# An HGRN2 layer on one core: block sums, a gate projection and residual steps in another place

## The chip, the core and the metric

The kernel runs on one core of one Trainium2 chip. A core has a matrix engine (TensorE, PE in the profile; its weight loads are listed apart as PEld), and VectorE (DVE), ScalarE (ACT), GpSimd (POOL) and SyncE (SP), which here issues all the transfers. Each engine takes its instructions in order from a queue of its own and waits on semaphores for the others. The metric is the device time of one execution in microseconds; lower is better.

## What is computed

A backbone of two layers over 512 latent tokens and 256 context tokens of width 1024. Layer 0 is a half-step SwiGLU, a bidirectional HGRN2 mixer and another half-step SwiGLU; layer 1 has a chunked MLP in the mixer's place. The change lies in the mixer of layer 0 and in the residual ahead of it:

```python
def post_norm_update(x, y, m, k, g, b):
    return layer_norm(DN_ALPHA * x + m[..., 3 * k + 2, :] * y, g, b)

def hgrn2_project(h, w_in, lb):
    p = (h @ w_in).astype(jnp.float32)
    p = p.reshape(bsz, length, 5, HG_HEADS, HG_DK).transpose(2, 0, 3, 1, 4)
    q = jax.nn.silu(p[0])
    i = p[1]
    lbb = lb[:, None]
    f = lbb + (1 - lbb) * jax.nn.sigmoid(p[2:4])
    return q, i, 1 - f, jnp.log(f), p[4]
...
    # gla_chunkwise, forward and reversed, over context and then latent tokens
    b = jnp.cumsum(logf, axis=-2)
    q_in = q * jnp.exp(b)
    k_in = k * jnp.exp(-b)
    scores = jnp.where(lower, jnp.einsum('nbhtd,nbhsd->nbhts', q_in, k_in), 0.0)
    o_intra = jnp.einsum('nbhts,nbhse->nbhte', scores, v)
...
    o = o * lax.rsqrt(jnp.mean(o * o, axis=-1, keepdims=True) + RMS_EPS) * norm_w
    o = o * jax.nn.silu(g)
```

`q` are the queries, `p[2:4]` the two forget gates (one for each direction), `i` the values and `g` the output gate, for each of 8 heads of width 128.

## The kernel before

**Precision and operands.** Every large product is made of three matmuls (`mm3`, L152 to L154): each operand is held as a high half, rounded by ScalarE (`split`, L139), and a low half, the difference, made by VectorE (L140). So a weight block costs one ACT and one DVE step beside its load. `unit` (L145) loads a block of 512 KB into one of three buffers `raw` and splits it into one of six buffers `w`. The features lie on the partitions: `xa` holds the 768 tokens for the mixer, the latent ones first.

**Values.** All values of the mixer (`i` above) are made ahead of the heads, by `HgrnValues`: a product of 2 x 2 blocks by seven block products in place of eight. The input is cut into four blocks, (feature half, token half), each 512 features by 384 tokens. Four of the products take sums of them, f5, f6, f7 and f4, in this order, and weights that are sums as well (`e`, `u`). `rest` (L984 on) makes these four products; each `next(steps)` in it emits the next of the sums, which `sum_steps` (L854 on, of a class shared with another phase) adds in place in `held`: one block addition is two DVE adds (L863), one sum's operand is two splits. L990 and L996 add products into values, L998 makes the last weight sums. Ahead of them stand the projections of head 0 to its queries and its gate (`proj_silu`, L1495 to L1505: 24 matmuls into `psq`, three ACT steps and a DVE product).

**Heads.** The loop over heads (from h = 0) works on two heads at once: it projects for head h and runs the scores and states of head h - 1. `proj_forget` (L1560 on) makes one direction's gates: `psfl` for the latent and `psfc` for the context tokens, clipped into `X` (L1568, L1569), then a chain to and fro between ScalarE and VectorE: L1575 (ACT), two logarithms, the differences L1576 and L1577 (DVE), the running sum by a scan (L1581), small steps, six L1594 (DVE) and L1595 (ACT) that finish `X`, the scaled keys, and L1597 (DVE), L1598 (ACT), L1605 (DVE, `queries`) that finish the scaled queries in `B`. TensorE then transposes the keys (`ptk`, L1611), makes the near scores (`pssn`, L1623, eight instances of 128 by 128, which read the queries and `kkn`), the far scores (`pssc`, L1634), the context states (`pkc`, L1643, read by DVE at L1650), the latent ones and the outputs (`po`, L1696 on). The transposes ahead of head 0's scores take the context keys of both directions first.

**Residual.** The input of post_norm_update for the mixer is x1 = ALPHA * (z1 * g + b), the output of the first half-step's layer norm, and is needed again only behind the mixer. `settle` (L1714 on) makes it at h = 0 right behind the first forget projection: for each half of the 1024 features a row load of g and of b (L1719, L1720), then for each of four token tiles a load of z (L1723), two DVE steps (L1724, L1725) and a store (L1726). The rows lie in the two buffers `kT` of the heads, z in their three `tmp`.

**Order.** The order of each engine's queue is decided when the kernel is built: a scheduler orders the instructions by their dependencies, buffers and the order in which the code emits them. A load into a buffer waits for the last reader of what lay there, and as SyncE's queue is in order, all transfers behind it wait too.

Of the kernel before, what the change touches and what calls it, by code (L numbers as in the profile page):

```python
# [19 lines left out]
P = 128  # L20
D = 1024
KD = D // P
T = 512
# [51 lines left out]
def backbone_kernel(  # L75
# [804 lines left out]
            put(self.f4, (0, 0))  # L880
            yield

    class HgrnValues(BothSums, Phase):


        hold = False
# [75 lines left out]
        def fifth(self):  # L962

            for c in range(2):
                nc.vector.tensor_tensor(self.e[c], self.g0[c], self.u[0][c], ALU.subtract)
            self.we = [self.weights(e) for e in self.e]

        def rest(self, steps):

# [526 lines left out]
    def proj_silu(h, idx, tag):  # L1496

        w = unit(hg_wf[idx, h])
        ps = bank("psq")
        last = feat_mm(ps, w, xm, 0, T)  # L1500
        o = qg.tile([P, T], F32, tag=tag, name=tag, bufs=1)
        nc.scalar.activation(o, ps, AF.Exp, scale=-1.0)
        nc.scalar.activation(o, o, AF.Ln, bias=one)
        nc.scalar.activation(o, o, AF.Exp, scale=-1.0)
        nc.vector.tensor_tensor(o, ps, o, ALU.mult)  # L1505
        return o, last

    with sbuf(name="vs", bufs=1) as vs:
        hv.f7, hv.f4, hv.f6, hv.f5 = (vs.tile([P, 2, KD // 2, TS], F32R, name=f"f{i}") for i in (7, 4, 6, 5))
        q0, g0 = proj_silu(0, 0, "q"), proj_silu(0, 3, "g")  # L1510
        hv.rest(hv.sum_steps())
    vw.close()

    with sbuf(name="hgo", bufs=1) as hgo, ExitStack() as late:
        hts = [hgo.tile([P, 2, T], F32R, name=f"ht{h}") for h in range(NH - NLATE)]
        hgo2 = late.enter_context(swap("hgo2"))
        hts.extend(hgo2.tile([P, 2, T], F32R, name=f"ht{h}") for h in range(NH - NLATE, NH))

        with sbuf(name="hg", bufs=1) as hg:
            mask = []  # L1520
            for d in range(2):
# [189 lines left out]
                lambda t: x1[t], True, (0, 2), None, lambda t: x2[t], f2, tail=4,  # L1711
            )

            def settle():  # L1714

                for hf in range(2):
                    c = slice(hf * HC, (hf + 1) * HC)
                    g, b = (hg.tile([P, NT, P], F32, tag="kT", name="kT", bufs=2).rearrange("p s t -> p (s t)") for _ in range(2))
                    nc.sync.dma_start(g, ln_g[0, 0][c].partition_broadcast(P))  # L1719
                    nc.sync.dma_start(b, ln_b[0, 0][c].partition_broadcast(P))  # L1720
                    for t in range(NT):
                        z = hg.tile([P, NT, P], F32, tag="tmp", name="z", bufs=3).rearrange("p s t -> p (s t)")
                        nc.sync.dma_start(z, z1[t][:, c])  # L1723
                        nc.vector.scalar_tensor_tensor(z, z, ALPHA, g, ALU.mult, ALU.mult)  # L1724
                        nc.vector.scalar_tensor_tensor(z, b, ALPHA, z, ALU.mult, ALU.add)  # L1725
                        nc.sync.dma_start(x1[t][:, c], z)  # L1726

            prev, made_of, g, last = None, None, None, None
            for h in range(NH + 1):
                if h < NH:  # L1730
                    n0, last, _ = proj_forget(h, 0)
                    if h == 0:
                        settle()
                else:
                    op.lead(0, 1)
                done = None
                if made_of:
                    with tc.issue_after(last.ins):
                        done = (made_of[0], outputs(*made_of), g)
                if prev:  # L1740
                    r0, r1 = prev
                    kTc = transposed([r.kk[:, NT + s, :] for r in prev for s in range(NTC)])
                    kT0 = transposed([r0.kk[:, s, :] for s in lat_order(0)[:-1]])
                    near_scores(r0)
                    far_scores(0, r0)
                if h < NH:
                    n1, _, last = proj_forget(h, 1)
                if done and h < NH:
                    with tc.issue_after(last.ins):
                        gated(*done)  # L1750
                if prev:
                    context_states(h - 1, prev, kTc)
                    kT1 = transposed([r1.kk[:, s, :] for s in lat_order(1)[:-1]])
                    latent_states(h - 1, 0, r0, kT0)
                    far_scores(1, r1)
                if h < NH:
                    q, last = proj_silu(h, 0, "q") if h else q0
                    if prev:

                        with tc.issue_after(last.ins):  # L1760
                            latent_states(h - 1, 1, r1, kT1)
                    for r in (n0, n1):
                        queries(r, q)
                else:
                    latent_states(h - 1, 1, r1, kT1)
                    op.lead(0, 2)
                    gated(*done)
                if prev:
                    made_of = (h - 1, prev)
                    if h == NH:  # L1770
                        on = outputs(*made_of)
                    g, last = proj_silu(h - 1, 3, "g") if h > 1 else g0
                if h < NH:
                    prev = (n0, n1)
# [271 lines left out]
```

## Time and profile before

| | us |
|---|---|
| three runs | 2413.31, 2415.90, 2416.14 (median 2415.9) |
| the profiled execution | 2413.81 |
| its span, first to last instruction | 2412.1 |
| mean granted TensorE clock | 0.998 |

The same, by stretches around the place of the change: length, busy time of TensorE, VectorE, ScalarE, granted clock, share of the transfer engines.

| stretch | us | PE | DVE | ACT | clock | DMA |
|---|---|---|---|---|---|---|
| plain value products, 500 to 560 | 60 | 59.17 | 47.11 | 23.09 | 1.00 | 0.32 |
| q and g of head 0, start of f5's and f6's, 560 to 587 | 27 | 27.00 | 26.60 | 22.09 | 1.00 | 0.13 |
| the other value products, forget gates of head 0, 587 to 637 | 50 | 50.00 | 35.75 | 20.93 | 1.00 | 0.59 |
| transposes and near scores of head 0, 637 to 651 | 14 | 6.10 | 11.64 | 7.01 | 0.76 | 0.37 |
| heads 0 and 1, 651 to 700 | 49 | 48.78 | 43.53 | 22.77 | 1.00 | 0.15 |

A row of the profile reads: start and duration in us of one instruction or of a run of the same ones, engine, line, operation, output and inputs by their names in the program, shape, count. What stands in brackets behind it is how long the engine idled just before and what released it: the engine, the tile and its line. A row without a start is a group: busy time, mean in ns, then idle before it. DMA issues are listed with their count, KB of each, and the median us from issue to landing.

### The profile page before, as it was taken

The numbers are of one execution on the slowest core, as the hardware profiler recorded it, in microseconds if no ns is written. First come the engines' busy times: TensorE is split into PE (matmuls) and PEld (weight loads), VectorE is DVE, ScalarE is ACT, GpSimd is POOL, SyncE is SP. The second block draws the span as 40 slices with busy tenths as digits, with TensorE's granted clock in tenths as the row PEclk, the third lists the DMA queues.
The fourth block names the chain that finished last, engine by engine and source line by source line (L and its number), as shares of the span: only waits on it lengthen the run. The fifth ranks groups of instructions, "written<-read, shape, count | busy, mean of one in ns | idle before, by whom it ended". The sixth has DMA issues, their size and how long they took to land.

```text
span 2412.1 us, 37626 instructions
## 1 busy us (share of the span) xinstructions
PE 2378.3 (99%) x14791; PEld 2183.0 (91%) x14791; DVE 2011.2 (83%) x3203; ACT 1197.3 (50%) x1861; POOL 35.6 (1%) x58
## 2 busy tenths in 40 slices
PE   7999999999899999999999999999999999999998
PEld 5899998888788988999988999889999988999987
DVE  7997797868788887988897988898888787988785
ACT  4544433336445443555534655544666543555641
POOL 0000000000000000000000000000000000000000
PEclk9999999999999999999999999999999999999999
DMA  7443489842411224433584333673332374333451
GB/s 302 169 162 125 137 293 379 289 159 82 151 57 52 63 62 147 138 106 106 176 263 155 106 106 115 202 227 135 99 103 88 123 251 151 132 109 105 146 164 73
DMA packets 110196, 362.05 MB, mean 150 GB/s; under 512 B 12681, under 2 KB 14913, under 8 KB 110018
## 3 DMA queue, kind: packets, MB, share of 16 engines
q1 hardware_dynamic: 110018, 359.65, 44.3%
q8 instruction: 115, 1.88, 0.3%
q14 instruction: 63, 0.52, 0.1%
HBM read 336.25 MB, written 23.36 MB: 149 GB/s over the span
## 4 chain that ended last, share of the span: by engine, by line
PE 87%; DVE 7%; DMA 2%; ACT 1%; issue 1%; POOL 0%; SPq 0%; DVEq 0%; POOLq 0%; ACTq 0%
PE y L152 9%; PE y L153 9%; PE y L154 9%; PE psc L152 7%; PE psc L154 7%; PE psc L153 7%; PE pse L154 3%; PE pse L152 3%; PE pse L153 3%; PE psa L152 2%; PE psa L154 2%; PE psa L153 2%; PE psf L152 2%; PE psf L154 2%; PE psf L153 2%; DVE w L140 1%
## 5 line engine op out<-in xcount | busy, mean ns | idle before, releaser
L139 ACT ACTIVATE w<-raw 128x1024 fp32r<-128x1024 f32 (+3 forms) x391 | 369.9, 949 | 377.8 <-DMA raw<-in_ffn_w_out 142.1
L140 DVE TENSOR_TENSOR w<-raw,w 128x1024 fp32r<-128x1024 f32 (+3 forms) x391 | 424.4, 1089 | 101.0 <-ACT w L139 100.4
L152 PE MATMUL y<-w,hs 128*128 128x512 f32 x976 | 380.7, 390 | 0.0
L154 PE MATMUL y<-w,hs 128*128 128x512 f32 x976 | 379.8, 389 | 0.0
L153 PE MATMUL y<-w,hs 128*128 128x512 f32 x976 | 379.8, 389 | 0.0
L152 PEld LDWEIGHTS y<-w,hs 128*128 128x128 f32 x976 | 183.2, 188 | 38.3
L154 PEld LDWEIGHTS y<-w,hs 128*128 128x128 f32 x976 | 183.2, 188 | 38.3
L153 PEld LDWEIGHTS y<-w,hs 128*128 128x128 f32 x976 | 183.2, 188 | 37.4
L152 PE MATMUL psc<-f,w 128*128 128x256 f32 (+1 forms) x680 | 199.1, 293 | 0.0
L154 PE MATMUL pse<-f,w 128*128 128x256 f32 (+1 forms) x680 | 198.9, 292 | 0.1
L152 PE MATMUL pse<-f,w 128*128 128x256 f32 (+1 forms) x680 | 198.7, 292 | 0.2 <-ACT sc L770 0.2
L153 PE MATMUL pse<-f,w 128*128 128x256 f32 (+1 forms) x680 | 198.6, 292 | 0.0
L154 PE MATMUL psc<-f,w 128*128 128x256 f32 (+1 forms) x680 | 198.5, 292 | 0.0
L153 PE MATMUL psc<-f,w 128*128 128x256 f32 (+1 forms) x680 | 198.5, 292 | 0.0
L770 ACT ACTIVATE sc<-psc 128x256 f32<-128x256 f32 (+1 forms) x235 | 94.6, 402 | 148.3 <-PE psc L154 136.7
L152 PE MATMUL psc<-xm,w 128*128 128x256 f32 x548 | 156.3, 285 | 1.6 <-ACT sc L770 1.6
L154 PE MATMUL psc<-xm,w 128*128 128x256 f32 x548 | 155.1, 283 | 0.0
L153 PE MATMUL psc<-xm,w 128*128 128x256 f32 x548 | 155.0, 283 | 0.0
L140 DVE TENSOR_TENSOR w<-rawu,w 128x1024 fp32r<-128x1024 f32 x85 | 103.9, 1223 | 46.8 <-ACT w L139 46.8
L152 PEld LDWEIGHTS psc<-f,w 128*128 128x128 f32 x680 | 130.0, 191 | 0.8 <-ACT sc L770 0.6
L154 PEld LDWEIGHTS pse<-f,w 128*128 128x128 f32 x680 | 130.0, 191 | 0.7 <-DVE w L140 0.7
L152 PEld LDWEIGHTS pse<-f,w 128*128 128x128 f32 x680 | 130.0, 191 | 0.4 <-ACT sc L770 0.4
(441 smaller groups left out, 6152.1 us busy)
## 6 DMA issues: line engine op xcount, KB each, us to landing
raw<-in_ffn_w_in SPq DMA_DIRECT2D x114, 512.0 KB, 4.6
raw<-in_ffn_w_out SPq DMA_DIRECT2D x88, 512.0 KB, 4.4
rawu<-in_ffn_w_in SPq DMA_DIRECT2D x75, 512.0 KB, 3.5
rawu<-in_mod_w SPq DMA_DIRECT2D x72, 512.0 KB, 4.2
mraw<-in_mod_w SPq DMA_DIRECT2D x56, 512.0 KB, 4.8
hl<-hd SPq DMA_DIRECT2D x44, 384.0 KB, 5.5
raw<-in_hg_wf SPq DMA_DIRECT2D x32, 512.0 KB, 3.9
x<-x SPq DMA_DIRECT2D x28, 512.0 KB, 4.1
```

Of the source, the lines that this page charges most:

```text
L139: latest_hi[0] = nc.scalar.activation(dst_hi, src, AF.Copy)
L140: latest[0] = nc.vector.tensor_tensor(dst_lo, src, dst_hi.bitcast(F32), ALU.subtract)
L152: nc.tensor.matmul(ps, ah, bh, start=start, stop=False, **kw)
L153: nc.tensor.matmul(ps, ah, bl, start=False, stop=False, **kw)
L154: return nc.tensor.matmul(ps, al, bh, start=False, stop=stop, **kw)
L770: self.copies.append(nc.scalar.activation(sc[i], ps[:, :N2], AF.Copy, scale=scale))
```

## The change

Three parts, all around the values and head 0. The line numbers of the changed kernel are higher by 24 to 29 behind the first part: L863 is L977 in the new function, L1568 is L1594, L1576 is L1602, L1594 is L1620, L1724 and L1725 are L1748 and L1749.

```diff
-    class HgrnValues(BothSums, Phase):
+    class HgrnValues(Phase):
...
+        def sum_steps(self):
...
+            add((1, 1), (0, 1))
+            put(self.f5, (1, 1))
+            yield
+            add((0, 1), (0, 0))
+            add((0, 0), (1, 1))
+            put(self.f6, (0, 0))
+            yield
+            add((1, 0), (0, 0))
+            put(self.f7, (1, 0))
+            yield
+            put(self.f4, (0, 1))
+            yield
...
-        q0, g0 = proj_silu(0, 0, "q"), proj_silu(0, 3, "g")
+        q0 = proj_silu(0, 0, "q")
         hv.rest(hv.sum_steps())
...
-        hgo2 = late.enter_context(swap("hgo2"))
-        hts.extend(hgo2.tile([P, 2, T], F32R, name=f"ht{h}") for h in range(NH - NLATE, NH))
...
-            def settle():
+            def settle(pool):
                 for hf in range(2):
                     c = slice(hf * HC, (hf + 1) * HC)
-                    g, b = (hg.tile([P, NT, P], F32, tag="kT", name="kT", bufs=2).rearrange("p s t -> p (s t)") for _ in range(2))
-                    nc.sync.dma_start(g, ln_g[0, 0][c].partition_broadcast(P))
-                    nc.sync.dma_start(b, ln_b[0, 0][c].partition_broadcast(P))
+                    g, b = (load_row(pool, f"r{n}{hf}", src[0, 0][c]) for n, src in (("g", ln_g), ("b", ln_b)))
                     for t in range(NT):
-                        z = hg.tile([P, NT, P], F32, tag="tmp", name="z", bufs=3).rearrange("p s t -> p (s t)")
+                        z = pool.tile([P, HC], F32, tag="z", name="z", bufs=4)
...
                     if h == 0:
-                        settle()
+                        with swap("st") as st:
+                            settle(st)
+                        hgo2 = late.enter_context(swap("hgo2"))
+                        hts.extend(hgo2.tile([P, 2, T], F32R, name=f"ht{h}") for h in range(NH - NLATE, NH))
...
                     q, last = proj_silu(h, 0, "q") if h else q0
+                    if h == 0:
+                        g0 = proj_silu(0, 3, "g")
```

`swap` opens a pool in the memory at the other end, which the values' weight sums (`ve`, `vu`) have left by then; the gated outputs of the last four heads (`hts`, pool `hgo2`) are placed there once settle's pool is closed. `load_row` (L275) allocates a row and loads it. Before, (0, 0) was added to first, and f5 stood on two block additions, of (0, 1) to (0, 0) and of (1, 1) to (0, 1).

Three places of the queues. First VectorE at the block sums, behind the plain value products; before, with f_4916 and f_4915 the operands of f5 and f6, f_4913 that of f7, `w<-ve` the weights of f5's product, and `lb`, `oml` small steps for the forget gates:

```order
L140 TENSOR_TENSOR w<-ve_4465,w 128x1024
L1490 TENSOR_SCALAR oml<-lb 128x16
L140 TENSOR_TENSOR w<-ve_4466,w 128x1024
L1505 TENSOR_TENSOR q<-psq,q 128x512
L140 TENSOR_TENSOR f_4916<-held,f_4916 128x768 x2
L863 TENSOR_TENSOR held<-held 128x2x384 x3
L1505 TENSOR_TENSOR g<-psq,g 128x512
L140 TENSOR_TENSOR f_4915<-held,f_4915 128x768 x2
L863 TENSOR_TENSOR held<-held 128x2x384
L140 TENSOR_TENSOR f_4913<-held,f_4913 128x768
```

The changed kernel from the first of the same weights on:

```order
L140 TENSOR_TENSOR w<-ve_4465,w 128x1024
L1514 TENSOR_TENSOR mx<-lbr 128x16
L140 TENSOR_TENSOR f_4916<-held,f_4916 128x768
L1515 TENSOR_TENSOR mx<-mx,lbr 128x16
L140 TENSOR_TENSOR f_4916<-held,f_4916 128x768
L1516 RECIPROCAL mx<-mx 128x16
L140 TENSOR_TENSOR w<-ve_4466,w 128x1024
L1517 TENSOR_TENSOR lb<-lbr,mx 128x16
L977 TENSOR_TENSOR held<-held 128x2x384
L1519 TENSOR_SCALAR oml<-lb 128x16
L1534 TENSOR_TENSOR q<-psq,q 128x512
L977 TENSOR_TENSOR held<-held 128x2x384 x4
```

Ahead of these rows stand four adds of the sums before, and two in the changed kernel; the low halves of f5 stand around the second weight split, ahead of q instead of behind it; the product for g is gone from here. The adds for f6 follow behind q.

Second VectorE at the residual steps, before, from the second z on (`X` and `B` are direction 0's forget gate, `psfl` and `psfc` its products):

```order
L140 TENSOR_TENSOR w<-raw,w 128x1024 x2
L1724 SCALAR_TENSOR_TENSOR z<-z,kT 128x512
L1725 SCALAR_TENSOR_TENSOR z<-kT,z 128x512
L1568 TENSOR_SCALAR X<-psfl 128x512
L1569 TENSOR_SCALAR X<-psfc 128x256
L1724 SCALAR_TENSOR_TENSOR z<-z,kT 128x512 x2
L1725 SCALAR_TENSOR_TENSOR z<-kT,z 128x512 x2
L1577 TENSOR_TENSOR X<-X,L 128x768
L1724 SCALAR_TENSOR_TENSOR z<-z,kT 128x512
L1576 TENSOR_TENSOR B<-B,L 128x768
L1725 SCALAR_TENSOR_TENSOR z<-kT,z 128x512
L1581 SCALAR_TENSOR_TENSOR B<-held,B 128x768
```

And the changed kernel, from the end of the first half of settle on:

```order
L1748 SCALAR_TENSOR_TENSOR z<-z,rg_5343 128x512 x2
L1749 SCALAR_TENSOR_TENSOR z<-rb_5345,z 128x512 x2
L1748 SCALAR_TENSOR_TENSOR z<-z,rg_5343 128x512
L1749 SCALAR_TENSOR_TENSOR z<-rb_5345,z 128x512
L140 TENSOR_TENSOR w<-raw,w 128x1024 x2
L1594 TENSOR_SCALAR X<-psfl 128x512
L1595 TENSOR_SCALAR X<-psfc 128x256
L140 TENSOR_TENSOR w<-raw,w 128x1024
L1603 TENSOR_TENSOR X<-X,L 128x768
L1602 TENSOR_TENSOR B<-B,L 128x768
L1607 SCALAR_TENSOR_TENSOR B<-held,B 128x768
L1594 TENSOR_SCALAR X<-psfl 128x512
```

The first forget steps stood between the settle steps, the scan (L1581) right behind the last of them; now all sixteen steps and two weight splits stand ahead of L1594, and a third split behind L1595.

Third SyncE's queue at the same place, before (`raw<-in_hg_wf` are weight blocks of the heads, `x_84<-z` the stores):

```order
L145 DMA raw<-in_hg_wf 128x1024 x5
L1719 DMA kT<-in_ln_g 128x512
L1720 DMA kT<-in_ln_b 128x512
L1723 DMA z<-z_83 128x512 x3
L145 DMA raw<-in_hg_wf 128x1024
L1726 DMA x_84<-z 128x512
L145 DMA raw<-in_hg_wf 128x1024
L1726 DMA x_84<-z 128x512 x2
L1723 DMA z<-z_83 128x512
L145 DMA raw<-in_hg_wf 128x1024
L1723 DMA z<-z_83 128x512 x2
L1726 DMA x_84<-z 128x512
```

And the changed kernel:

```order
L145 DMA raw<-in_hg_wf 128x1024 x3
L275 DMA rg_5319<-in_ln_g 128x512
L275 DMA rb_5321<-in_ln_b 128x512
L1747 DMA z<-z_83 128x512 x4
L275 DMA rg_5343<-in_ln_g 128x512
L1750 DMA x_84<-z 128x512
L275 DMA rb_5345<-in_ln_b 128x512
L145 DMA raw<-in_hg_wf 128x1024
L1750 DMA x_84<-z 128x512 x3
L1747 DMA z<-z_83 128x512 x4
L145 DMA raw<-in_hg_wf 128x1024
L1750 DMA x_84<-z 128x512
```

All four z loads and both sets of rows are now issued behind one another, without a wait for a kT buffer; the second four z loads stand behind the stores of the first four, whose buffers they take, and the weight blocks that were issued between the z loads of the first half stand behind them.

More of the change, by code (lines that the diff above doesn't have):

```diff
@@ L966, in fifth, with block, add, put @@
             self.we = [self.weights(e) for e in self.e]
+        def sum_steps(self):
+            n = self.nk
+            def block(r, c, j):
+                return self.blk[:, r * n + 2 * j : r * n + 2 * j + 2, c * TS : (c + 1) * TS]
+            def add(x, y):
+                for j in range(2):
+                    nc.vector.tensor_tensor(block(*x, j), block(*x, j), block(*y, j), ALU.add)
+            def put(dst, x):
+                for j in range(2):
+                    ks = slice(2 * j, 2 * j + 2)
+                    split(dst[:, 0, ks, :], dst[:, 1, ks, :], block(*x, j))
+            add((1, 1), (0, 1))
[10 more added lines that the diff above has]
+            yield
         def rest(self, steps):
```

## Prediction

> **What bounds the kernel now.** The page comes first: engine totals, and the chain of work that ended last.
>
> ```profile
> span 2412.1 us, 37626 instructions
> PE 2378.3 (99%) x14791; PEld 2183.0 (91%) x14791; DVE 2011.2 (83%) x3203; ACT 1197.3 (50%) x1861; POOL 35.6 (1%) x58
> PE 87%; DVE 7%; DMA 2%; ACT 1%; issue 1%; POOL 0%; SPq 0%; DVEq 0%; POOLq 0%; ACTq 0%
> ```
>
> TensorE is busy nearly everywhere, and the chain runs through it, so a change can win only its idle time and its clock. Next, what TensorE waited for (total, times, longest):
>
> ```profile
> PE ptk L1611 <- ACT X L1595: 6.8, 1, 6.8
> ...
> PE psc L152 <- ACT sc L770: 1.6, 3, 0.7
> PE pssn L1623 <- DVE B L1605: 1.1, 1, 1.1
> ```
>
> The largest single wait of the program and the one of 1.1 us stand in the stage that the change rewrites. The rows left out belong to the first 31 us, but for one of 0.8 at 555.1, ahead of the stage; of what comes later than 650.1, 0.7 is the longest. The timeline of TensorE in the stage (start, duration), the same steps one head later (from 679.72), and two windows, in which the granted clock stands behind the busy times:
>
> ```profile
> 637.45 0.71 PE L1611 MATMUL ptk<-ident,X 128*128 128x128 f32 x5
> 644.95 0.69 PE L1611 MATMUL ptk<-ident,X 128*128 128x128 f32 x2 [6.79 <-ACT X L1595]
> 646.74 2.04 PE L1623 MATMUL pssn<-B,kkn 128*128 128x128 f32 x8 [1.10 <-DVE B L1605]
> 650.10 0.48 PE L152 MATMUL psfl<-xa,w 128*128 128x512 f32 x1
> 679.72 1.06 PE L1623 MATMUL pssn<-B,kkn 128*128 128x128 f32 x8
> 681.43 0.47 PE L152 MATMUL psfl<-xa,w 128*128 128x512 f32 x1
> 640.00:643.50 3.50, 0.00 (x0) 0.00 (x0) 3.50 (x10) 0.21 (x1) 0.00 (x0) 0.96 0.17 18
> 643.50:650.00 6.50, 3.95 (x17) 3.58 (x18) 4.20 (x8) 5.09 (x8) 0.00 (x0) 0.50 0.45 153
> ```
>
> The reader is to see two losses. TensorE idles 6.79 + 1.10 = 7.89 us. And after the idle the granted clock is 0.50, so that the scores from pssn to the next psfl last 650.10 − 646.74 = 3.36 us, where one head later they last 681.43 − 679.72 = 1.71: another 1.65 us, which the waits don't show.
>
> The Trainium skill, "TensorE: Matmul & The Clock Gate", section "What's actually happening", states this as a rule: after an idle window of about 3.4 us the clock is halved, until TensorE has been busy again for about as long. The trace agrees: 0.96 up to 643.5, 0.50 behind it.
>
> **Why TensorE waits there.** The transposes ptk need X of both directions of head 0, and X comes out of a chain that goes to and fro between VectorE (DVE) and ScalarE (ACT). Their timelines:
>
> ```profile
> 607.59 0.69 DVE L1724 SCALAR_TENSOR_TENSOR z<-z,kT 128x512 f32<-128x512 f32 x1 [0.17 <-DMA z<-z]
> 620.96 0.42 DVE L1569 TENSOR_SCALAR X<-psfc 128x256 f32<-128x256 f32 x1 [2.18 <-PE psfc L154]
> 623.08 1.29 DVE L1724 SCALAR_TENSOR_TENSOR z<-z,kT 128x512 f32<-128x512 f32 x2 [1.69 <-DMA kT<-in_ln_b]
> 629.01 1.75 DVE L1581 TENSOR_TENSOR_SCAN B<-held,B 128x768 f32<-128x768 f32 x1
> 633.05 0.68 DVE L1597 TENSOR_TENSOR B<-B,sm 128x512 f32<-128x512 f32 x1
> 634.59 0.68 DVE L1725 SCALAR_TENSOR_TENSOR z<-kT,z 128x512 f32<-128x512 f32 x1
> 639.26 1.75 DVE L1581 TENSOR_TENSOR_SCAN B<-held,B 128x768 f32<-128x768 f32 x1
> 642.26 1.66 DVE L1594 SCALAR_TENSOR_TENSOR X<-B,X 128x128 f32<-128x128 f32 x6
> 620.96 1.06 ACT L139 ACTIVATE w<-raw 128x1024 fp32r<-128x1024 f32 x1 [6.77 <-PE psfc L154]
> 623.76 1.03 ACT L1575 ACTIVATE B<-B,one,lb 128x768 f32<-128x768 f32 x1
> 643.96 0.94 ACT L1595 ACTIVATE X<-X,lnoml 128x768 f32<-128x768 f32 x1 [1.36 <-DVE X L1594]
> 644.80 0.61 ACT L1598 ACTIVATE B<-B 128x512 f32<-128x512 f32 x1
> ```
>
> The chain starts at 620.96 and delivers the second X at 643.96 + 0.94 = 644.90. Within it stand eight of the sixteen settle steps (L1724, L1725), 0.60 apart (two take 1.29), and a wait of 1.69 for the second set of row loads, which had to wait for the kT buffers of the first.
>
> **The change: the gate projection.** Its 24 matmuls move behind both forget projections of head 0; their time doesn't vanish.
>
> ```profile
> 560.68 0.39 PE L152 MATMUL psq<-xa,w 128*128 128x512 f32 x1
> 571.56 0.39 PE L152 MATMUL pve<-w,f 128*128 128x512 f32 x1
> L863 DVE TENSOR_TENSOR held<-held 128x768 f32<-128x768 f32 x8 | 7.4, 948 | 0.0
> L140 DVE TENSOR_TENSOR f<-held,f 128x768 fp32r<-128x768 f32 x8 | 7.4, 956 | 0.0
> L140 DVE TENSOR_TENSOR w<-ve,w 128x1024 fp32r<-128x1024 f32 x4 | 4.9, 1224 | 0.0
> ```
>
> The two projections, 48 matmuls, take 10.88 us (0.227 each), so 24 take 5.44: the value products start at 566.1, and the forget projections 5.44 us earlier than before. Behind both of them the 5.44 come back. Without a new wait TensorE thus reaches ptk at 637.45, as before, but with forget results that are 5.44 us older. That alone wins nothing unless DVE keeps up.
>
> **The block sums.** They have to be ready 5.44 us earlier. Their number stays (eight adds, eight low halves); f5 needs two adds ahead of it instead of four. From DVE's last step before them, which ends near 562.65: two adds (1.90), a weight split (1.22), two low halves (1.91) give 567.7, with small steps about 567.8. TensorE wants the second low half of f5 for its 11th matmul, 566.1 + 10 × 0.227 = 568.4. For f6 follow a weight split, six adds, the product for q and two low halves, near 576.9; it is wanted for f6's 13th matmul, 566.1 + 48 × 0.227 = 577.0. So no wait, and little cover: one more split in front would cost 1.2 us. Bounds 0 and 1.2; I take 0, the nearer one, since both sums come out ahead.
>
> **Settle in memory of its own.** All sixteen steps now stand ahead of the first forget step, so the end E of settle decides when the chain starts.
>
> ```profile
> 586.75 2.36 DVE L998 SCALAR_TENSOR_TENSOR ve<-raw,ve 128x1024 f32<-128x1024 f32 x2
> 599.47 0.38 SPq L1719 DMA_DIRECT2D kT<-in_ln_g  x1
> raw<-in_hg_wf SPq DMA_DIRECT2D x9, 512.0 KB, 4.6
> z<-z SPq DMA_DIRECT2D x8, 256.0 KB, 3.5
> x<-z SPq DMA_DIRECT2D x8, 256.0 KB, 2.0
> ```
>
> SyncE issues the row loads right behind two weight loads that wait for the L998 steps. Those come some 1.3 to 2 us earlier, as the gate's weight split (1.22) and product stood ahead of them; the second ends near 587.8 and the rows go out near 588.3. In the first kernel, with the same loads ahead, the first settle step ran 607.59 − 599.47 = 8.1 us after that issue; so now at 596.4. Eight steps and two L996, 0.60 apart, and one duration end at 602.5. The second four z loads need the stores of the first four landed (2.0 each): they go out at 603.0 to 605.2, and with 3.5 to land the first is there at 606.5; two weight splits fill the time between. Eight steps of 0.60 and the tail give **E = 611.6**, an estimate from these rows. Bounds: from 587.8 DVE has four splits, three L990, an L996 and small steps ahead of settle, 7.2 us; with no wait for any load, settle would end at 595.0 + 18 × 0.60 + 2 × 1.14 = 608.1. If the second set waits 8.1 us from its issue as the first did, it ends at 603.0 + 8.1 + 4.9 = 616.0.
>
> From E on: last store and weight issue 0.5; landing 4.6; the weight split to L1575 as from 620.96 to 624.79, 3.8; DVE's L1576 (an add of 0.95), then scan to L1597 as from 629.01 to 633.73, and L1569, together 5.9; for direction 1 the same four ACT steps and the rest of direction 0's, 4.5; L1576, scan, a split and the six L1594 (639.26 to 643.92), 5.9; L1595 and L1598, 1.5; L1605, 0.7; to TensorE 0.1. The sum is 27.5: pssn at 639.1. TensorE by itself would be there at 637.45 + 7 × 0.11 = 638.2 (five transposes take 0.71, so 0.11 apart). So 0.9 us of wait remain of 7.89, with the clock at 1.00. psfl of head 1 then starts at 639.1 + 1.71 = 640.8 instead of 650.10: **9.3 us less**.
>
> What is late next is DVE, about 2.2 us later against TensorE's now faster scores. Its cover:
>
> ```profile
> 658.72 0.42 DVE L1569 TENSOR_SCALAR X<-psfc 128x256 f32<-128x256 f32 x1 [1.83 <-PE psfc L154]
> 659.62 0.29 DVE L1650 COPY S<-pkc 128x128 f32<-128x128 f32 x1 [0.47 <-PE pkc L1643]
> ```
>
> DVE idles 1.83 and 0.47 there, 2.30 in all, so it is level again before the states of head 0 are wanted. Without that cover up to 2.2 us would be given back at the next transposes. Behind this place both programs have one order, and no wait of TensorE is above 0.7, so the gain lasts to the end.
>
> **Sum.** The profiled execution took 2413.81 us (span 2412.1 and 1.7 around it): 2413.8 − 9.3 = 2404.5. The median of the three runs, 2415.9, stands 2.1 above it, so for a median I give 2406.6.
>
> **Rivals.** *Full cover*: the loads land early, E is at most 610.7, and TensorE never waits. psfl starts at 638.2 + 1.71 = 639.9: 10.2 us less, 2405.7. For it: the least E is 608.1. Against it: the 8.1 us of the first rows.
>
> *Partial*: the second set of loads is as slow as the first, E = 616.0, pssn at 643.5, psfl at 645.2: 4.9 us less, 2411.0. For it: the second rows kept DVE waiting 1.69 before. By the clock rule of the Trainium skill an idle of 643.5 − 638.2 = 5.3 us would halve the clock again, which would make 2412.7.
>
> *Slower*: settle keeps its pace of before, from 599.47 to 635.27, 35.8 us from the first row load to the last step. Then E = 588.3 + 35.8 = 624.1, pssn starts at 651.6, lasts with the scores 3.36 at half clock, and psfl starts at 655.0: 4.9 us later than before, 2420.8. Since every forget step now stands behind all of settle, each microsecond of E counts in full; it turns from E = 650.10 − 3.36 − 27.5 = 619.2 on. Against it: much of that pace was DVE's order, with forget steps between the halves, and the two kT buffers.
>
> *The sums don't come earlier*: with four adds ahead of f5 it would be ready at 569.7, 1.3 us after TensorE wants it. The order of the adds speaks against that, and such a wait comes first out of the 0.9 that remain at ptk: 2407.0.
>
> **How the numbers follow.** Forecast, with the late sums, 60%; full cover 22%; partial 13%; slower 5%. A measurement of this kernel can tell 0.2%, 4.8 us, from no change: forecast and full cover lie beyond it (0.82), partial at its edge and counted as same (0.13), slower 0.05. The range takes in full cover, somewhat widened for the 2.8 us by which the three runs differ, and partial in between its two prices: 2404.0 to 2412.0.
>
> **What would show it.** Right: ptk near 637.5 with under 2 us of idle before its last two and pssn; pssn about 1.06 long and the clock 1.00 from 640 to 650; psfl of head 1 near 641; the last settle step near 611.6. Wrong: a wait of TensorE on f5 or f6 above 1.2; settle ending behind 616; idle ahead of ptk above 3 us or a clock of 0.50 between 640 and 650; or a gain there that goes again at po or later.

## The result and the profile after

Over 15 runs each, the changed kernel takes 2410.32 us (median; 2407.89 to 2411.99) and the kernel before 2414.07 (2412.46 to 2416.14): a ratio of 0.9983, with a 95% interval of 0.9975 to 0.9991. The gain is 3.75 us, clear of the noise, and less than half of the 9.3 that were forecast. The profiled execution took 2409.93 us, its span is 2408.2, 3.9 shorter than that of before. The page of the changed kernel, the lines that answer to those shown of before:

```profile
span 2408.2 us, 37612 instructions
PE 2379.6 (99%) x14791; PEld 2184.0 (91%) x14791; DVE 2011.5 (84%) x3203; ACT 1197.3 (50%) x1861; POOL 35.6 (1%) x58
```

No engine's number of instructions changed, and no busy time by more than 1.3 us. What changed are TensorE's two waits in the stage (what it waited for; total, times, longest), which were 6.8 and 1.1:

```profile
PE ptk L1637 <- ACT X L1621: 2.8, 1, 2.8
...
PE pssn L1649 <- DVE B L1631: 0.2, 1, 0.2
```

TensorE's timeline in the stage, and the two windows of before that held the idle time, with the granted clock behind the busy times:

```profile
637.67 0.38 PE L1637 MATMUL ptk<-ident,X 128*128 128x128 f32 x2
640.83 1.33 PE L1637 MATMUL ptk<-ident,X 128*128 128x128 f32 x5 [2.78 <-ACT X L1621]
642.36 2.04 PE L1649 MATMUL pssn<-B,kkn 128*128 128x128 f32 x8 [0.20 <-DVE B L1631]
645.76 0.77 PE L152 MATMUL psfl<-xa,w 128*128 128x512 f32 x1
640.00:643.50 3.50, 2.47 (x10) 2.10 (x11) 3.46 (x6) 3.48 (x6) 0.00 (x0) 0.54 0.23 95
643.50:650.00 6.50, 6.50 (x29) 5.77 (x28) 5.02 (x7) 2.52 (x4) 0.00 (x0) 0.72 0.23 81
```

The reader is to see two things. TensorE reaches ptk at 637.67, as forecast, but waits 2.78 us there. And the clock falls to half all the same: near scores start at 642.36 instead of 639.1, they and the far scores take 645.76 − 642.36 = 3.40 us instead of 1.71, and even the first matmuls of psfl are slow (0.77 against 0.48).

The chain of work that ended last, followed through the stage (start, duration, what), tells where the rest of the wait comes from (rows under 0.1 us left out):

```profile
603.45 0.32 SPq L1750
603.86 4.93 DMA z<-z
608.81 0.70 DVE z L1748
...
613.42 0.70 DVE z L1749
614.14 0.32 SPq L1750
614.55 4.98 DMA raw<-in_hg_wf
619.61 1.06 ACT w L139
620.67 0.74 ACT B L1598
```

The second half of the residual steps waits for its z loads; SyncE issues those behind the last store of the first half. The last step ends at 613.42 + 0.70 = 614.1, its store goes out, and only then the load of a weight block, 4.98 us. ScalarE's queue has the split of that block (619.61) ahead of the first exponential of the forget chain (L1598), whose product TensorE had finished at 615.7. VectorE's clips of that product (L1594 at 618.55, L1595 at 619.15) stand behind splits as well, of the two blocks ahead of this one, for which ScalarE waited 5.57 and 0.87 us.

### The profile page after: what moved, and what is told of

The parts are those of the page before. It is cut to its first block, busy times and chain, and to the rows that moved or that the text cites. A ratio compares the mean times of both kernels' runs of the same rounds, so it can differ in the third digit from the quotient of the medians.

```text
span 2408.2 us, 37612 instructions
## 1 busy us (share of the span) xinstructions
PE 2379.6 (99%) x14791; PEld 2184.0 (91%) x14791; DVE 2011.5 (84%) x3203; ACT 1197.3 (50%) x1861; POOL 35.6 (1%) x58
## 4 chain that ended last, share of the span: by engine, by line
PE 89%; DVE 6%; ACT 2%; DMA 1%; issue 1%; POOL 0%; SPq 0%; DVEq 0%; POOLq 0%; ACTq 0%
PE y L154 9%; PE y L153 9%; PE y L152 9%; PE psc L152 7%; PE psc L154 7%; PE psc L153 7%; PE pse L154 4%; PE pse L152 4%; PE pse L153 4%; PE psf L152 2%; PE psf L154 2%; PE psf L153 2%; PE psa L154 2%; PE psa L153 2%; PE psa L152 2%; PE psq L152 1%
```

## The experiments

The first theory (A) is the forecast's: the forget chain starts behind the last residual step, so near scores come a fixed time behind it. The rivals are named with each run; theory C is put in other words from run to run, and comes in the end to this: the chain waits for weight blocks, whose loads the residual's transfers hold back. The traces are compared by distances from the start of q's projection, which each of them has at about 561, to three points: the first near score (pssn), the next forget product (psfl), and that gate's first context product (psfc of head 1), where the clock is whole again in all of them. From psfc to TensorE's last matmul the traces take 1746 to 1750 us, where the programs are the same but for the residual steps that some of them have there, so single times tell 2 us apart at best. The distances are much finer: those of the one kernel that was traced twice agree within 0.02 us.

| kernel | q at | to pssn | to psfl | to psfc | ratio to before (95%) |
|---|---|---|---|---|---|
| before | 560.68 | 86.06 | 89.42 | 94.97 | |
| changed | 560.84 | 81.52 | 84.92 | 91.08 | 0.9983 (0.9975 to 0.9991) |
| gate alone | 561.07 | 82.43 | 85.84 | 92.46 | 0.9983 (0.9974 to 0.9993) |
| residual alone | 561.51 | 82.79 | 85.95 | 91.51 | 0.9995 (0.9985 to 1.0004) |
| changed, old sums | 561.19 | 81.42 | 84.82 | 91.60 | 0.9974 (0.9964 to 0.9985) |
| changed, filler | 561.22 | 82.12 | 83.90 | 89.43 | 0.9970 (0.9958 to 0.9982) |
| changed, loads first | 560.88 | 81.84 | 85.25 | 92.09 | 0.9980 (0.9971 to 0.9989) |
| changed, steps spread | 561.22 | 77.65 | 79.42 | 84.98 | 0.9962 (0.9948 to 0.9976) |
| before, steps spread | 561.01 | 82.77 | 86.18 | 92.26 | 0.9990 (0.9980 to 0.9999) |
| transfers only | 561.22 | 81.22 | 84.54 | 90.11 | 0.9985 (0.9976 to 0.9994) |
| steps only | 561.07 | 77.59 | 79.36 | 84.92 | 0.9955 (0.9940 to 0.9969) |
| residual on GpSimd's queue | 560.78 | 79.20 | 80.98 | 86.55 | 0.9968 (0.9956 to 0.9981) |
| steps spread, old sums | 561.24 | 78.43 | 80.21 | 85.76 | 0.9965 (0.9953 to 0.9978) |
| steps spread, again | 560.77 | 77.65 | 79.42 | 85.00 | 0.9962 (0.9949 to 0.9976) |

### The parts alone

The first part without the others:

```diff
-        q0, g0 = proj_silu(0, 0, "q"), proj_silu(0, 3, "g")
+        q0 = proj_silu(0, 0, "q")
...
                     q, last = proj_silu(h, 0, "q") if h else q0
+                    if h == 0:
+                        g0 = proj_silu(0, 3, "g")
```

> The kernel before with the first part alone: the gate projection of head 0 behind both forget projections; sums and residual steps as before. Theory A (the chain that starts behind the residual steps sets when TensorE gets its keys; the gate move only matters through it): the residual steps come 1.3 to 2 us earlier, with the second set of row loads still waiting for the kT buffers, so near scores start 1 to 1.7 us earlier than 646.74, with TensorE's wait ahead of them still above 5 us: 1 to 1.7 us less than before, a ratio of 0.9993 to 0.9996. Theory B (the gate move is what gives the gain, the rest is nothing): about 3.9 us less, ratio 0.9984.

Near scores came 86.06 − 82.43 = 3.6 us earlier, not 1 to 1.7, and 2.5 of it were left at psfc. The row loads of the residual, in the kernel with the gate move alone, show where it comes from:

```profile
595.26 0.42 SPq L1719 DMA_DIRECT2D kT<-in_ln_g  x1
```

Before, the same row stood at 599.47: 4.2 us earlier, or 4.6 against q. The value products themselves moved up by 4.6 us against q (5.4, less a wait for f5 with the old sums), and the weight blocks that SyncE issues ahead of the rows wait until those products release the buffers of their splits (ScalarE starts such a split, when a value product lets it, at 590.79 instead of 594.97). Only VectorE's smaller load had been counted, not what TensorE's earlier products release.

The third part without the others (`settle(pool)` and its pool as in the diff, gate and sums as before):

> The kernel before with the third part alone: residual steps in memory of their own. Theory A: the row loads go out near 589.5 instead of 599.47, the last residual step ends near 615.5 (changed kernel: 614.1), near scores start 28 us behind it, near 643.7, and the next forget projection near 647.1 instead of 650.10: about 3.0 us less, ratio 0.9988. Theory B: no change, ratio 1.000.

Near scores came 3.3 us earlier, as theory A had it (3.0), and psfc 3.5. In time the interval runs from 3.6 us less to 1.0 more, so the times alone don't separate it from nothing; the trace does. The two parts alone win 3.6 and 3.3 us at the near scores, both together 4.6 (86.06 − 81.42, with the old sums): they shorten the same wait, and something else ends it from there on.

The changed kernel without the second part:

```diff
-    class HgrnValues(Phase):
+    class HgrnValues(BothSums, Phase):
```

> The changed kernel with the old order of the block sums: gate and residual parts without the second part. Theory A: TensorE waits about 1.3 us for the low half of f5's sum, which comes out of the 2.98 us that it waits ahead of the scores anyway, as long as the residual steps do not move: 0 to 1.3 us more than the changed kernel, 2410.3 to 2411.6 (ratio to the kernel before 0.9984 to 0.9990). Theory B (the sums are what makes the gate move worth anything): the 3.75 us are lost, ratio 1.000.

TensorE waits for f5 there, and it doesn't matter. Its largest waits in this kernel, among others:

```profile
PE ptk L1608 <- ACT X L1592: 1.9, 1, 1.9
...
PE pve L152 <- ACT f L139: 0.6, 1, 0.6
```

The 0.6 us come out of the wait at ptk, 1.9 instead of 2.8; the distance to the near scores is the same (81.42 and 81.52). At psfc the kernel without it is 0.5 us later (91.60 and 91.08). Its time came out lower than expected, 2408.3 us for 2410.3 to 2411.6, a ratio of 0.9974 beside 0.9983 of the changed kernel, but the intervals overlap. So in the changed kernel the second part wins nothing that shows in the time, and at most 0.5 us in the trace.

### The clock

```diff
                 for i, blk in enumerate(blocks):
+                    if i == 2:
+                        for _ in range(fill):
+                            nc.tensor.transpose(pt[:, 3 * P : 4 * P], ident, ident)
                     nc.tensor.transpose(pt[:, i * P : (i + 1) * P], blk, ident)
...
-                    kTc = transposed([r.kk[:, NT + s, :] for r in prev for s in range(NTC)])
+                    kTc = transposed([r.kk[:, NT + s, :] for r in prev for s in range(NTC)], 22 if h == 1 else 0)
```

> The changed kernel with 22 extra transposes of a constant between the second and the third key transpose of head 0, in the 2.78 us in which TensorE waits; they write where the last of these transposes writes over them, so the output is the same. Theory A (the clock falls to half because TensorE stands still there): they take 2.4 us and end before the keys come, the granted clock stays at 1.00 from 640 to 647, near scores and far scores take 1.7 us instead of 3.40, the first context product of the forget gate (psfc) starts at 649.6 instead of 651.92: 2.3 us less than the changed kernel, about 2408. Theory B (the scores are slow there for another reason, their operands coming late): no change, 2410.3, or up to 0.5 more.

TensorE's timeline with the filler (L1639), and the window over its wait and the scores:

```profile
638.26 2.57 PE L1639 MATMUL ptk<-ident 128*128 128x128 f32 x22
641.82 0.77 PE L1640 MATMUL ptk<-ident,X 128*128 128x128 f32 x5 [0.99 <-ACT X L1621]
643.34 1.13 PE L1652 MATMUL pssn<-B,kkn 128*128 128x128 f32 x8 [0.76 <-DVE B L1631]
645.12 0.48 PE L152 MATMUL psfl<-xa,w 128*128 128x512 f32 x1
643.30:647.00 3.70, 3.66 (x24) 3.40 (x25) 2.94 (x4) 3.61 (x6) 0.00 (x0) 1.00 0.30 94
```

The clock stays at 1.00 and the scores take 645.12 − 643.34 = 1.78 us, with operands that came 0.6 us later than in the changed kernel (why, was not looked into). To psfc the distance falls from 91.08 to 89.43, 1.65 us in spite of them. So theory B fell, and of the forecast's 9.3 us some 2.3 (3.40 instead of 1.71 at the scores, 6.16 instead of 5.53 from psfl to psfc) went to the clock.

### What ends the wait

Theory A says the last residual step. To bring it forward, all its loads were issued ahead:

```diff
+                rows = [[load_row(pool, f"r{n}{hf}", src[0, 0][hf * HC : (hf + 1) * HC]) for n, src in (("g", ln_g), ("b", ln_b))] for hf in range(2)]
...
+                        z = hg.tile([P, NT, P], F32, tag=tag, name="z", bufs=n).rearrange("p s t -> p (s t)")
+                    zs.append(z)
+                    nc.sync.dma_start(z, z1[i % NT][:, i // NT * HC : (i // NT + 1) * HC])
+                for i, z in enumerate(zs):
...
```

> The changed kernel with all loads of the residual steps issued ahead: both sets of rows and the first four z first, the second four z into buffers of the heads, so that they do not wait for stores. Theory A (near scores follow about 28 us behind the last residual step): that step ends near 611.3 instead of 614.1, near scores start near 639.6 instead of 642.36, TensorE waits under 1 us and its clock stays at 1.00, so the context products of the next forget gate (psfc) start near 646.8 instead of 651.92: about 5 us less than the changed kernel, 2405. Theory C (the loads crowd each other: the rows and z collide with the weight loads behind them): the last residual step comes earlier, but the weights of the forget gates land later by as much, and the scores stay at 642: 2410.

Theory A fell here. VectorE's and ScalarE's timelines of this kernel:

```profile
610.25 1.28 DVE L1755 SCALAR_TENSOR_TENSOR z<-rb,z 128x512 f32<-128x512 f32 x2
618.23 1.06 ACT L139 ACTIVATE w<-raw 128x1024 fp32r<-128x1024 f32 x1 [5.36 <-DMA raw<-in_hg_wf]
620.92 0.85 ACT L1598 ACTIVATE B<-X 128x768 f32<-128x768 f32 x1 [0.32 <-DVE X L1595]
```

The last residual step ends at 611.53, 2.6 us earlier, as meant; the forget chain's first exponential starts at 620.92 and not at 618, as 6.5 us behind that step, the changed kernel's distance, would be. ScalarE stands 5.36 us before a weight block, and VectorE's clip L1595, which the exponential needs, stands behind the split of it (theory C).

Then the residual steps out of head 0, two (half, tile) units behind the forget gates of each of heads 1 to 4:

```diff
-                    if h == 0:
-                        with swap("st") as st:
-                            settle(st)
...
+                    with tc.issue_after(latest[0].ins), tc.issue_after(latest_load[0].ins):
+                        if h == 1:
+                            pool = st.enter_context(swap("st"))
+                            rows = settle_rows(pool)
+                        if 1 <= h <= 4:
+                            settle(pool, rows, 2 * h - 2)
+                            settle(pool, rows, 2 * h - 1)
...
```

The gated outputs of the last heads (`hgo2`) are then placed at head 5.

> The changed kernel with the residual steps out of head 0: two of the eight (half, tile) units behind the forget gates of each of heads 1 to 4. Theory A: the chain of the forget gates then starts when their first product is there, 3.4 us earlier; near scores start near 639 instead of 642.36, wait under 1 us, clock 1.00, psfc of the next head near 646 instead of 651.92: 6 us less, of which heads 1 to 4 may give back 0 to 4, as VectorE has 2.4 us more to do in each and idles 5.4 of 49 us there: 2404 to 2408, ratio to the kernel before 0.996 to 0.9975. Theory C (the chain is held by the weight loads and splits, not by the residual steps): scores at 641 to 642, 2409 to 2411, or more with what heads 1 to 4 lose.

It came out as theory A had it, and at the size of the forecast. Theory C, which here had the weight loads late even without the residual, had 641 to 642 and missed. But the run takes the steps and the stores behind them out together, so it doesn't tell which of them held the chain; loads remain in the stretch (four rows and four z from 594.86 on), stores don't. VectorE's first forget step on the context product, and TensorE behind it:

```profile
616.12 0.42 DVE L1595 TENSOR_SCALAR X<-psfc 128x256 f32<-128x256 f32 x1 [2.18 <-PE psfc L154]
638.05 0.93 PE L1637 MATMUL ptk<-ident,X 128*128 128x128 f32 x7
638.87 1.13 PE L1649 MATMUL pssn<-B,kkn 128*128 128x128 f32 x8
640.64 0.48 PE L152 MATMUL psfl<-xa,w 128*128 128x512 f32 x1
```

VectorE now waits for TensorE at L1595, not TensorE for VectorE; there is no wait at ptk or pssn, and psfl of head 1 starts at 640.64, where the forecast had 640.8 for the changed kernel. Heads 1 to 4 give nothing back that shows: 2405.3 us, beside 2414.8 of the kernel before in the same comparison.

The same spreading with gate and sums in their old places:

> The kernel before with only the residual steps spread over heads 1 to 4 in the same way: gate projection and block sums in their old places. Theory A: the forget products then come 5.4 us later than in the changed kernel, the first context product ends at 620.9, near scores start about 23 us behind it, near 644, after a wait of some 5 us, and at half clock; psfc of the next head near 652.5 instead of 655.65: 3 us less than the kernel before, ratio 0.9987. So the gate move is worth 6 us when the residual steps are gone, against about 1 beside them. Theory D (TensorE's wait is only VectorE's load in this stretch, wherever the products stand): the wait is gone here too, and the time is that of the spread kernel with the gate moved.

Near what was expected: pssn at 643.78 after waits of 3.51 and 1.10, and 2.7 us less than before at psfc (94.97 − 92.26), for 3. So theory D fell: where the products stand matters. With the residual gone from head 0, gate move and sums are worth 92.26 − 84.98 = 7.3 us; beside it, 91.51 − 91.08 = 0.4.

Now the two halves of the residual apart. First its transfers alone; VectorE's two steps for each tile are left out, so x1 is z unscaled:

```diff
-                        nc.vector.scalar_tensor_tensor(z, z, ALPHA, g, ALU.mult, ALU.mult)
-                        nc.vector.scalar_tensor_tensor(z, b, ALPHA, z, ALU.mult, ALU.add)
                         nc.sync.dma_start(x1[t][:, c], z)
```

> The changed kernel without the sixteen residual steps of VectorE: each z is loaded and stored as it is, so the scaling of the residual by ln_g and ln_b is left out; the row loads, z loads and stores stay on SyncE's queue in head 0. Theory C (the forget chain is held by weight blocks whose loads stand behind the residual's transfers on SyncE's queue and share the transfer engines with them): near scores stay at 641 to 643, clock at half, 2409 to 2411. Theory A (it is held by the end of the residual steps on VectorE): without them the near scores start near 639 without a wait, as in the spread kernel, 2405.

Then its VectorE steps alone, on a tile of ones ahead of the first forget step, in the kernel with the steps spread:

```diff
+                            with tc.issue_after(first[0].ins):
+                                for _ in range(8):
+                                    nc.vector.scalar_tensor_tensor(d0, d0, ALPHA, d1, ALU.mult, ALU.mult)
+                                    nc.vector.scalar_tensor_tensor(d0, d1, ALPHA, d0, ALU.mult, ALU.add)
```

> The spread kernel with sixteen steps of the same kind and size put into head 0 on VectorE, on a tile of ones and without any transfer, ahead of the first forget step; what they make isn't used. Theory C: VectorE has idle time for them between 594 and 616, the weights come as in the spread kernel, and near scores start at 638.9 to 639.6: 2405 to 2406. Theory A: the steps end near 613 and the near scores follow 28 us behind them, near 641, at half clock: 2409.

VectorE ahead of and at the first forget steps, and ScalarE's split that it waits for, with the transfers only (three rows); then VectorE with the steps only (three rows):

```profile
614.58 1.06 ACT L139 ACTIVATE w<-raw 128x1024 fp32r<-128x1024 f32 x1 [6.16 <-DMA raw<-in_hg_wf]
615.67 1.22 DVE L140 TENSOR_TENSOR w<-raw,w 128x1024 fp32r<-128x1024 f32 x1 [14.35 <-ACT w L139]
619.68 0.42 DVE L1595 TENSOR_SCALAR X<-psfc 128x256 f32<-128x256 f32 x1
```

```profile
610.93 0.68 DVE L1771 SCALAR_TENSOR_TENSOR d<-d,d 128x512 f32<-128x512 f32 x1
613.11 0.69 DVE L1597 TENSOR_SCALAR X<-psfl 128x512 f32<-128x512 f32 x1 [1.49 <-PE psfl L154]
615.98 0.42 DVE L1598 TENSOR_SCALAR X<-psfc 128x256 f32<-128x256 f32 x1 [2.18 <-PE psfc L154]
```

With no residual steps to do, VectorE idles 14.35 us for ScalarE's split of a weight block, and ScalarE 6.16 us for the block; the near scores stand where they stood (81.22). With all sixteen steps to do, but without the stores and loads that go with them, VectorE is ready before TensorE, and the distance is 77.59, that of the spread kernel (2403.6 us, under the 2405 to 2406 expected, within the noise). So the residual's transfers alone are enough to hold the chain, and its arithmetic alone costs nothing.

Two things limit this. Without the steps the queue has another order: behind the first rows no weight block goes out before 610.47, where the changed kernel issues two by then (600.01 and 608.63), so that 81.22 lies so near 81.52 may be chance in part. And in the changed kernel the steps act through the stores, which wait for them: the block behind the last store goes out when the last step is done.

That leaves two ways in which they hold it: as weight loads queue behind them on SyncE, or as they share the transfer engines. So z loads and stores on another queue:

```diff
-                        nc.sync.dma_start(z, z1[t][:, c])
+                        nc.gpsimd.dma_start(z, z1[t][:, c])
...
-                        nc.sync.dma_start(x1[t][:, c], z)
+                        nc.gpsimd.dma_start(x1[t][:, c], z)
```

> The changed kernel with the z loads and the stores of the residual issued by GpSimd in place of SyncE, so that no weight load stands behind them; VectorE's steps stay. Theory C with the queue's order as the cause: the weight blocks come when their buffers are free, the first forget step starts near 616, near scores near 639 to 640, clock 1.00: 2405 to 2406.5. Theory C with the sharing of the transfer engines as the cause: the weights land late all the same, near scores at 641 to 642: 2409. Theory A: as the residual steps end no sooner than 614, near scores at 642: 2410. If GpSimd's transfers come later than SyncE's, the residual steps and with them the scores come later than in the changed kernel.

ScalarE's split ahead of the first exponential, in the changed kernel (one row); then VectorE's last residual step, the same split, the first forget step and TensorE's near scores with GpSimd's queue:

```profile
619.61 1.06 ACT L139 ACTIVATE w<-raw 128x1024 fp32r<-128x1024 f32 x1 [2.24 <-DMA raw<-in_hg_wf]
```

```profile
615.39 0.69 DVE L1749 SCALAR_TENSOR_TENSOR z<-rb,z 128x512 f32<-128x512 f32 x1
615.70 1.07 ACT L139 ACTIVATE w<-raw 128x1024 fp32r<-128x1024 f32 x1 [6.76 <-PE psfc L154]
617.14 0.69 DVE L1594 TENSOR_SCALAR X<-psfl 128x512 f32<-128x512 f32 x1
639.98 1.13 PE L1649 MATMUL pssn<-B,kkn 128*128 128x128 f32 x8 [0.75 <-DVE B L1631]
```

The last residual step ends at 616.1, 2.0 us later than in the changed kernel, and the near scores come 2.3 us earlier (79.20 against 81.52), at a clock of 1.00. The split waits for TensorE now, and not for its block: from 595 to 622 us ScalarE idles 0.6 us for weight blocks, where it is 15.1 in the changed kernel, though the transfer engines are nearly as busy (share 0.77 and 0.81 from 595 to 610; from 608.8 to 620 it is 0.84 and 0.98). So it is mainly the queue's order: with no weight load behind the stores, the weights are there. That sharing adds a part is not excluded. GpSimd also issues the first z loads 4 us sooner (585.40), which was not taken apart; the last step comes no sooner for it. The residual steps then do bind: 639.98 − 616.08 = 23.9 us from the last of them to the near scores. The rest to the spread kernel, 1.5 us, was not taken apart further.

### The sums where nothing covers them

The spread kernel with the old sums, and the spread kernel again beside it:

> The spread kernel with the old order of the block sums. Theory A (the sums decide when TensorE can start the block products once those come right behind q): TensorE waits 0.6 us for f5 as in the changed kernel with the old sums, and as it waits nowhere behind that, the 0.6 us stay to the end: near scores 0.6 us later against the start of q's projection than in the spread kernel, whose distance is 638.87 - 561.22 = 77.65. Theory B (later sums are made good): the same distance. The times can't tell 0.6 us apart.

> The spread kernel again, beside it on the same chip: 2405 us, a ratio to the kernel before of 0.996, and the same distance of 77.65 us from the start of q's projection to the near scores as in its first run.

The distances are 78.43 and 77.65: with no later wait to cover it, the second part is worth 0.8 us, of which 0.6 is the wait for f5. The spread kernel repeats: its distances to 0.02 us, and its ratio is 0.9962 both times (2405.45 us beside 2415.27 in the second). Of the complete kernels without idle work it is the fastest that was run; the one with the sixteen useless steps, 0.9955, is level with it within the intervals.

## Why the forecast was right in sign and wrong in size

- **What bounds the kernel.** Right: the whole gain was in TensorE's wait and clock in this stage (3.9 us at psfc, 3.9 in the span), and nothing was given back later.
- **The gate projection.** TensorE reached ptk where forecast (637.67 for 637.45). That the move "alone wins nothing unless DVE keeps up" overlooked that it brings DVE's own chain forward: alone it won 3.6 us at the near scores, since the value products, 4.6 us earlier there, also release weight buffers and so SyncE's queue earlier.
- **The block sums.** Right: no wait for f5 or f6. The price of the rival was 1.3 us; measured 0.6, out of the wait at ptk as the rival said.
- **E, the end of the residual steps.** 611.6 was forecast; measured 614.1. The first row loads and the first eight steps were right within 1 us (first step 597.0 for 596.4). The second four z failed: they went out at 603.86 for 603.0, and took 4.93 us to land, where 3.5, the median of all such loads, had been taken. The transfer engines were busy with stores and a weight block beside them (share 0.87 from 603.8 to 608.8); that this made them slow is likely and was not tested by itself. A load in such a stretch had to be priced between that median and the 8.1 of the first rows.
- **From E on.** 27.5 us were forecast, 28.2 measured (642.36 − 614.12), and so the sum came out nearly right; but it isn't a constant, as the run with the loads first (31.2) and the one with GpSimd's queue (23.9) show. The weight load behind the last store (0.5 + 4.6) was in the sum as a step of the chain, and not seen as the thing that holds it; that blocks issued before it come late as well was not in the sum.
- **The clock.** The sum took 1.00, as the wait left over was to be 0.9 us. It was 2.78, and the half clock of before came back with its whole price: 1.7 us at the scores and 0.6 at psfl. Of the signs of being wrong that the prediction names, this one came, a clock of 0.50 between 640 and 650 (640.3 to 647.1); the idle time, 2.78 + 0.20 us, and E stayed inside theirs.

In terms of the sum, at psfc: 2.5 (E) + 0.7 (behind E) + 2.3 (clock) = 5.5 of the 9.3 us missing, and 3.9 measured. Of the rivals, "partial" came nearest: it had near scores at 643.5, psfl at 645.2 and, at half clock, 3.2 us less (2412.7 from 2415.9); measured 642.36, 645.76 and 3.75. It had a chance of 13%; what told for it, z loads as slow as the first ones, was in the profile.

That the time, 2410.3, lies inside the stated range of 2404.0 to 2412.0 is luck in part. The range was worked out from a median of 2415.9 over three runs of the kernel before, and over 15 runs that median is 2414.07; a gain of 3.75 us from 2415.9 would have ended at 2412.15, just outside.

## What to carry to other kernels

When work is moved off an in-order chain, look at what its transfers stand in front of on the issuing queue: sixteen vector steps by themselves cost nothing here, while their loads and stores held back weight blocks that everything behind needed. Take the landing time of a load from a stretch that is as busy as the one it will run in, not from the median. And two edits that end the same wait don't add: find what is late next by removing the suspect entirely, as the spread kernel did, before pricing what remains.

## What the hardware did that was not expected

The granted clock fell after shorter waits than the idle window of about 3.4 us from which the forecast reasoned. The stretches at 0.50, in windows cut at the fall and the rise of the clock: of the changed kernel, of the one with the old sums, and of the one with the residual part alone:

```profile
638.10:640.20 2.10, 0.00 (x0) 0.00 (x0) 2.10 (x9) 0.57 (x2) 0.00 (x0) 1.00 0.48 117
640.30:647.00 6.70, 5.97 (x24) 5.41 (x25) 5.21 (x10) 5.70 (x9) 0.00 (x0) 0.50 0.31 112
```

```profile
639.20:641.80 2.60, 0.72 (x5) 0.53 (x5) 2.60 (x8) 1.70 (x4) 0.00 (x0) 1.00 0.69 202
641.90:648.60 6.70, 5.99 (x22) 5.54 (x23) 5.17 (x9) 4.35 (x6) 0.00 (x0) 0.50 0.26 78
```

```profile
639.00:643.70 4.70, 0.44 (x2) 0.20 (x2) 4.67 (x14) 3.34 (x6) 0.00 (x0) 1.00 0.06 23
643.80:647.10 3.30, 2.80 (x13) 2.83 (x14) 1.00 (x3) 2.81 (x5) 0.00 (x0) 0.50 0.50 159
```

In the changed kernel it fell 2.2 us after the last matmul (638.05 to 640.2); with the old sums TensorE had idled only 1.92 us and had been working again for 0.7 when it fell. Before, it fell 5.1 us after the last matmul (638.15 to 643.2). All of this agrees with windows of fixed length that don't start with the idle time, and that count as idle when TensorE was busy for less than about half: in the 3.4 us ahead of the fall it had been busy for some 1.2 and 1.5 us. A wait of 1.2 us in two pieces, with GpSimd's queue (0.47 and 0.75), did not make it fall. The stretch at half clock lasted 6.8 us in these two and 3.4 in the third, where TensorE was at work through most of it (2.80 of 3.30). The Trainium skill, "TensorE: Matmul & The Clock Gate", section "What's actually happening", has free-running windows of 3413 ns too, and the 6.8 and 3.4 us agree with two and one of them; that such a window needs to be only about half idle fits these traces, and was not tested by itself. If it is so, where these windows fall can make a difference of about 1 us between kernels with much the same wait: the residual part alone and the changed kernel are 1.3 us apart at the near scores and 0.4 at psfc.
